# A hybrid attention and convolution layer on one core: V and the third pattern's results in other layouts, and another order at the end of the first attention stretch

## The chip, the cores and the metric

The kernel runs on one core of a Trainium2 chip. The metric is the time of one execution on the device in microseconds (us), lower is better. The core has a matmul engine (TensorE, PE in the profile), a vector engine (VectorE, DVE), a scalar engine (ScalarE, ACT), a general engine (GpSimd, POOL) and a queue that starts transfers (SyncE, SP). ScalarE and GpSimd can start transfers too.

## The reference, cut to what matters

One encoder layer on 2048 positions of width 1024. After a norm, one projection gives queries, keys and values for 8 attention heads of size 64, and two halves for a gated convolution. Each head attends within three patterns (windows of 128 positions at stride 1, 512 at stride 4, 2048 at stride 16), and the three results are weighed by their softmax denominators:

```python
def dilated_sliding_attention(q, k, v):
    outs, lses = [], []
    for window, d in ((128, 1), (512, 4), (2048, 16)):
        half = window // (2 * d)
        o, lse = banded_attention(to_strided(q, d), to_strided(k, d), to_strided(v, d), half)
        outs.append(from_strided(o, d, B)); lses.append(from_strided(lse, d, B))
    w = softmax(stack(lses, axis=0), axis=0)
    return sum(w[..., None] * stack(outs, axis=0), axis=0)

h = x + concat([att, conv]) @ w_out          # att: 8 heads, conv: 31 taps, norm, silu
h = h + cross_attention(rmsnorm(h), rmsnorm(mem))
h = h + square(relu(rmsnorm(h) @ w_up)) @ w_down
out = rmsnorm(h)
```

## The kernel before

Float32 products are formed from high and low parts, three matmuls for each (`mm3`, lines 198 to 200). The work goes by groups of 512 positions (p = 0 to 3), except the projection, which is made for all groups first.

**Scratch in DRAM.** Values of all heads are stored by position (`vtok`, one row of 8 x 130 float16 for each position, with 256 rows of zeros ahead and behind that `edges`, line 711, writes from a tile of 16 partitions; that tile has the tag `raw`, as the weights' tiles have). The results of the second pattern (stride 4) and of the third (stride 16) are stored in `oscr[pair][0]` and `oscr[pair][1]`, a row of two heads by 66 numbers for each position: 64 sums, the denominator and the minimum.

**Attention.** `att_units` (line 948) yields units. A unit writes scores of four blocks of 128 queries and keys into a PSUM bank (kind `S`, L993 and L857), VectorE adds the mask and takes minima (L773), ScalarE takes exponentials (L774), TensorE turns them (L780), ScalarE and VectorE copy the high and low parts (ph L783, pl L784), and TensorE multiplies with V (L788 to L790). `att` (line 1048) runs the three stages of successive units beside one another. The third pattern spans all positions, so it is computed for all groups during group 0's attention (`att_far`, line 837), the *far stretch*; its order for each pair of heads is: head a third pattern, second, first; head b the same. For groups 1 to 3 a pair has first and second pattern only.

V tiles are single: v1 (first pattern, five transfers), v2 (second, eight transfers of 128 pieces), v3 (third, one transfer of 2048 pieces); in the far stretch all three are asked for at a pair's end.

`combine` (line 884) weighs the three results of a pair. It loads the two stored ones (`ld`, lines 889 to 891), waits some steps, and takes the common minimum on VectorE (csm, L904 and L905), exponentials on ScalarE, and the products and sums on GpSimd (L906 to L932). For the last pair of group 0 VectorE does them (`W = DVE if end else POOL`), and its result stays in SBUF as an input of the output projection; the others go through DRAM. `catT` (L940) turns the result. The call `after(st, "dve")` pins the first instruction behind the VectorE instruction written before it.

**The order.** Engines take their instructions in order. The kernel's order is made by generators: `weave(main, (side, rate))` runs `rate` steps of a side for each step of the main one; `pinned` keeps a generator's instructions behind the last one of an engine. A planner then places the instructions on the engines by estimated times. In the far stretch the gate projections of groups 2 and 3 (`rest`) run beside attention, 0.75 step for each attention step. Then group 0's `post` begins: `resid_linear` (line 1182) multiplies the eight chunks of w_out; chunks 0 to 2 run together over inputs 4 to 7 (convolution), 0 and 1, then 2 and 3 (attention pairs), so that the last pair's result is needed last. Their first six steps run beside the last attention units:

```python
    for p in range(NG):
        main = post(p)
        if p == 0:
            weave(islice(pinned(main, "pe"), 6), (first, 2.4))
            drain(first)
        sides = [(att(p + 1), 0.95), (conv(cv, p + 1), 0.6)] if p + 1 < NG else []
        weave(main, *sides)
```

Of the kernel before, what the change touches and what calls it, by code (L numbers as in the profile page):

```python
# [10 lines left out]
F32 = mybir.dt.float32  # L11
# [36 lines left out]
def hybrid_layer(ctx, tc, A, out):  # L48
# [61 lines left out]
    vtok = dr.tile([256 + S + 256, VR], F16, name="vtok")  # L110
# [3 lines left out]
    oscr = [[dr.tile([S, 2 * ROW], F32, name=f"oscr{p}_{q}") for q in (1, 2)] for p in range(4)]  # L114
# [430 lines left out]
    def lin_v(g, ns):  # L545
# [18 lines left out]
        for t in range(4 * ns[0], 4 * ns[-1] + 4):  # L564
# [10 lines left out]
            s2 = st.rearrange("p h e -> p (h e)")  # L575
            gs = slice(g * 4 * VW, (g + 1) * 4 * VW)
            dma(vtok[256 + P * t:256 + P * (t + 1), gs], s2)
# [133 lines left out]
    def edges():  # L711
        zrow = wp.tile([16, 1, VR], F16, tag="raw", name="zrow", bufs=2)
        DVE.memset(zrow, 0.0)
        zb = zrow.to_broadcast([16, 16, VR])
# [122 lines left out]
    def att_far(p2_, h, k, vt, q):  # L837
# [5 lines left out]
        def unit(rq, qh, ql):  # L843
# [39 lines left out]

    def combine(p, pr, o0):

        if p:
            yield
        ld = aq.tile([P, 2, 4, 2, ROW], F32, tag="ld", name=f"ld{p}{pr}")
        for i in range(2):
            dma(ld[:, i].rearrange("p j h e -> p j (h e)"),  # L890
                oscr[pr][i][512 * p:512 * (p + 1)].rearrange("(j p) e -> p j e", p=P))
        yield
        yield
        if p == 0:
            for _ in range(2 if pr < 3 else 1):
                yield
# [3 lines left out]
        end = p == 0 and pr == H // 2 - 1  # L900
# [6 lines left out]
        for i in range(2):  # L907
            W.tensor_tensor(e3[:, 1 + i], mm_, ld[:, i, :, :, HD + 1], op=ALU.subtract)
# [6 lines left out]
        for i in range(2):  # L915
            W.tensor_tensor(d3[:, 1 + i], e3[:, 1 + i], ld[:, i, :, :, HD], op=ALU.mult)
# [8 lines left out]
        for i in range(3):  # L925
            W.tensor_tensor(e3[:, i], e3[:, i], d2, op=ALU.mult)
        at = aq.tile([P, 4, 2, HD], F32, tag="cat", name=f"cat{p}{pr}")
        for i in range(3):
            src = ld[:, i - 1, :, :, 0:HD] if i else o0[:, :, :, 0:HD]
            W.tensor_tensor(src if i else at, src, e3[:, i].unsqueeze(3).to_broadcast([P, 4, 2, HD]), op=ALU.mult)  # L930
            if i:
                W.tensor_tensor(at, at, src, op=ALU.add)  # L932
# [15 lines left out]
    def att_units(p, far, then):  # L948
# [8 lines left out]
        def load_v(pr, pats):  # L957
            es = slice(pr * 2 * VW, (pr + 1) * 2 * VW)
            if 2 in pats and far:
                vt[2] = far.tile([P, 16, 2 * VW], F16, tag="v3", name=f"v3_{pr}")  # L960
                dma(vt[2], vtok[256:256 + S, es].rearrange("(i r) e -> i r e", r=16))
            if 0 in pats:
                vt[0] = aq.tile([P, 5, 2 * VW], F16, tag="v1", name=f"v1_{p}{pr}")
                for c in range(5):
                    t0 = 256 + 512 * p + P * c - 64
                    dma(vt[0][:, c], vtok[t0:t0 + P, es].rearrange("(i r) e -> r i e", r=16))
            if 1 in pats:
                vt[1] = aq.tile([P, 4, 2, 2 * VW], F16, tag="v2", name=f"v2_{p}{pr}")
                for c in range(2):
                    src = vtok[512 * (p + c):512 * (p + c) + 512, es].rearrange("(i a b) e -> b a i e", a=4, b=4)  # L970
                    for b in range(4):
                        dma(vt[1][:, b, c], src[b])

        def unit(pr, hh, pat, g, k, q_, opt, o0):
# [28 lines left out]
            for z in range(2):  # L1003
                blk = 2 * g + z
                for c in range(2):
                    vv = vt[1][:, blk, c] if pat else vt[0][:, blk + c]
# [7 lines left out]
            if g and hh and pat:  # L1014
                dma(oscr[pr][0][512 * p:512 * (p + 1)].rearrange("(p b) e -> p b e", b=4),
                    os_.rearrange("p b h e -> p b (h e)"), POOL if far else nc.scalar)
# [11 lines left out]
        for pr in range(H // 2):  # L1028
            K = [load_keys(2 * pr + hh, p, hh) for hh in range(2)] if far else None
            o0 = aq.tile([P, 4, 2, ROW], F32, tag="o0", name=f"o0_{p}{pr}", bufs=2)  # L1030
            for hh in range(2):
                h = 2 * pr + hh
                if far:
# [3 lines left out]
                    yield from att_far(far, h, k, vt, q3)  # L1037
# [144 lines left out]
    def resid_linear(load, rhs, korder, resid, hs, ssum, key, y, name, steps=False):  # L1182


        for ms in ((0, 1, 2), (3,), (4,), (5,), (6,), (7,)):
            wt = [load(m) for m in ms]
            pts = {}
            for ks in (korder[0:4], korder[4:6], korder[6:8]) if len(ms) > 1 else (korder,):
                for m, (wh, wl) in zip(ms, wt):
                    if m not in pts:  # L1190
                        pts[m] = ps("mm", f"{name}{m}")
# [13 lines left out]
    def post(p):  # L1205
# [9 lines left out]
        def from_x(m):  # L1215
# [8 lines left out]
                                p == 0)  # L1224
# [211 lines left out]
```

## Time and profile before

| | |
|---|---|
| time, median of 3 runs | 2902.63 us (2901.68 to 2903.17) |
| the profiled execution | 2896.44 us; span 2894.6 us, mean granted clock 0.992 |
| TensorE, VectorE, ScalarE, GpSimd busy | 98%, 64%, 40%, 16% of the span |
| transfers | 433.73 MB, mean 150 GB/s |

The profiled execution has its own time beside the runs; the span is from the first instruction to the last. A group line reads: source line, engine, operation, out<-in by the program's names, shapes, count, then busy time and mean, then the engine's idle time before those instructions and who ended it. TensorE's idle time before an instruction stands in brackets in the timeline. The order of phases is: preparation and projections up to 540 us, the far stretch to about 770 us, and then `post` of group 0 with the attention and convolution of group 1 beside, and so on.

### The profile page before, as it was taken

What the parts mean: (1) busy time and instruction counts of PE and PEld (TensorE: products, weight loads), DVE (VectorE), ACT (ScalarE), POOL (GpSimd) and SP (SyncE); (2) the same over time, 40 slices, a digit from 0 to 9 for tenths busy, and PEclk for the clock granted to TensorE, in tenths of its full rate; (3) what the DMA queues carried; (4) which work ended last, traced back from release to release, by engine and by line L of the source; (5) the groups of instructions that cost most, each with busy time, mean ns of one, the idle gap of its engine ahead of it and who ended that gap; (6) DMA issues with size and microseconds to landing.
All of it is one profiled execution on the core that took longest, in us unless ns stands there. A gap on an engine that the chain in (4) does not pass through costs nothing.

```text
span 2894.6 us, 41429 instructions
## 1 busy us (share of the span) xinstructions
PE 2826.2 (98%) x15628; PEld 2377.7 (82%) x15628; DVE 1860.5 (64%) x3311; ACT 1167.0 (40%) x1988; POOL 472.7 (16%) x522
## 2 busy tenths in 40 slices
PE   8989999989899999999999999999999999999999
PEld 7878899878788888888888888888888888888888
DVE  5636536455689876566887756689877555544445
ACT  5623211466444343434543344445333433432233
POOL 1336431133002011200022012002111200000000
PEclk9999999999999999999999999999999999999999
DMA  8979854799834444545444546534543445233332
GB/s 259 295 157 228 200 146 134 178 232 237 219 98 127 142 132 126 170 145 164 124 124 128 146 116 192 175 100 121 143 127 115 139 131 175 90 93 100 97 95 73
DMA packets 606656, 433.73 MB, mean 150 GB/s; under 512 B 174886, under 2 KB 537434, under 8 KB 606457
## 3 DMA queue, kind: packets, MB, share of 16 engines
q1 hardware_dynamic: 566904, 408.81, 49.4%
q10 hardware_dynamic: 37952, 16.88, 2.3%
q0 software_dynamic: 1600, 5.41, 0.7%
q8 instruction: 123, 2.02, 0.3%
q14 instruction: 77, 0.62, 0.1%
HBM read 339.89 MB, written 91.11 MB: 149 GB/s over the span
## 4 chain that ended last, share of the span: by engine, by line
PE 84%; DVE 7%; DMA 4%; issue 2%; ACT 1%; SPq 1%; POOL 0%; POOLq 0%; DVEq 0%; ACTq 0%
PE dn L198 8%; PE dn L199 8%; PE dn L200 8%; PE up L198 8%; PE up L200 7%; PE up L199 7%; PE lin L198 4%; PE lin L200 3%; PE lin L199 3%; PE xs L198 2%; PE xs L200 2%; PE xs L199 2%; PE o L198 2%; PE o L199 2%; PE o L200 2%
## 5 line engine op out<-in xcount | busy, mean ns | idle before, releaser
L199 PE MATMUL dn<-hhl,whi_d 128*128 128x512 f32 (+1 forms) x1056 | 403.0, 384 | 1.4 <-DVE hhl L1310 1.4
L198 PE MATMUL up<-mh,whi_u 128*128 128x512 f32 x1024 | 402.6, 393 | 0.5 <-DVE rl L1307 0.5
L198 PE MATMUL dn<-hhh,whi_d 128*128 128x512 f32 (+1 forms) x1056 | 401.5, 391 | 1.1 <-ACT hhh L1309 1.1
L200 PE MATMUL dn<-hhh,wlo_d 128*128 128x512 f32 (+1 forms) x1056 | 402.1, 384 | 0.0
L199 PE MATMUL up<-ml,whi_u 128*128 128x512 f32 x1024 | 399.7, 390 | 1.6 <-DVE ml L1200 1.6
L200 PE MATMUL up<-mh,wlo_u 128*128 128x512 f32 x1024 | 399.8, 391 | 0.0
L215 DVE SCALAR_TENSOR_TENSOR cacc<-cu,cw,cacc 128x512 f32<-128x512 f32 x480 | 387.9, 808 | 5.5
L189 ACT CAST whi_d<-raw_d 128x1024 fp32r<-128x1024 f32 x128 | 134.6, 1052 | 424.8 <-PE up L199 380.0
L1325 DVE TENSOR_TENSOR h<-h,dn 128x512 f32<-128x512 f32 (+1 forms) x264 | 172.1, 666 | 161.8 <-PE dn L200 160.5
L189 ACT CAST whi_u<-raw_u 128x1024 fp32r<-128x1024 f32 x128 | 134.4, 1050 | 327.7 <-PE dn L199 299.6
L1307 DVE SCALAR_TENSOR_TENSOR rl<-up,ssumx 128x512 f32<-128x512 f32 x128 | 87.9, 690 | 260.6 <-PE up L200 256.4
L198 PEld LDWEIGHTS dn<-hhh,whi_d 128*128 128x128 f32 x1056 | 197.8, 188 | 40.7 <-DVE h L1325 3.5
L200 PEld LDWEIGHTS dn<-hhh,wlo_d 128*128 128x128 f32 x1056 | 198.4, 188 | 39.4
L199 PEld LDWEIGHTS dn<-hhl,whi_d 128*128 128x128 f32 x1056 | 198.8, 188 | 37.6 <-DVE hhl L1310 2.3
L199 PEld LDWEIGHTS up<-ml,whi_u 128*128 128x128 f32 x1024 | 192.5, 188 | 40.8 <-DVE ml L1200 3.0
L200 PEld LDWEIGHTS up<-mh,wlo_u 128*128 128x128 f32 x1024 | 192.3, 188 | 40.1
L198 PEld LDWEIGHTS up<-mh,whi_u 128*128 128x128 f32 x1024 | 192.4, 188 | 38.6 <-DVE rl L1307 0.9
L774 ACT ACTIVATE sm<-sm,o 128x256 f32<-128x256 f32 (+1 forms) x384 | 160.1, 465 | 121.8 <-DVE o L773 121.5
L190 DVE TENSOR_TENSOR wlo_u<-raw_u,whi_u 128x1024 fp32r<-128x1024 f32 x128 | 161.6, 1262 | 26.7 <-ACT whi_u L189 26.5
L190 DVE TENSOR_TENSOR wlo_d<-raw_d,whi_d 128x1024 fp32r<-128x1024 f32 x128 | 161.2, 1260 | 23.5 <-ACT whi_d L189 23.4
L773 DVE CUSTOM_DVE_ANT_0 sm<-s,mask 128x256 f32<-128x256 f32 (+1 forms) x384 | 128.3, 374 | 61.2 <-PE s L993 33.8
L176 POOL TENSOR_TENSOR nr<-st_v,mhalf 128x4 f32<-128x4 f32 (+1 forms) x13 | 13.4, 1031 | 845.7 <-DVE st_v L172 845.7
(402 smaller groups left out, 6341.1 us busy)
## 6 DMA issues: line engine op xcount, KB each, us to landing
raw_u<-in_w_up_dram SPq DMA_DIRECT2D x128, 512.0 KB
raw_d<-in_w_down_dram SPq DMA_DIRECT2D x128, 512.0 KB
raw_o<-in_w_out_dram SPq DMA_DIRECT2D x32, 512.0 KB
raw_a<-ascr SPq DMA_DIRECT2D x32, 512.0 KB
raw_b<-bscr SPq DMA_DIRECT2D x32, 512.0 KB
v<-vtok SPq DMA_DIRECT2D x208, 65.0 KB
k<-kscr SPq DMA_DIRECT2D x24, 512.0 KB
k<-kscr SPq DMA_DIRECT2D x8, 1152.0 KB
```

Source lines behind the costliest of these rows:

```text
L176: POOL.tensor_tensor(dst, v, mhalf.to_broadcast([P, v.shape[1]]), op=ALU.pow)
L189: ACT.copy(hi, raw)
L190: (lo_eng or DVE).tensor_tensor(lo, raw, f(hi), op=ALU.subtract)
L198: PE.matmul(o, lh, rh, start=first, stop=False)
L199: PE.matmul(o, lh, rl, start=False, stop=False)
L200: last["pe"] = PE.matmul(o, ll, rh, start=False, stop=end)
L215: DVE.scalar_tensor_tensor(acc, u[:, t:t + 512], cw[:, c, t:t + 1], acc, op0=ALU.mult, op1=ALU.add)
L773: last["dve"] = DVE.tensor_tensor_reduce(dst, so, mask[:, 256 * m:256 * m + nk], 1.0, 3e38, ALU.add, ALU.min, mn)
L774: last["act"] = ACT.activation(dst, dst, AF.Exp, bias=mn, scale=-1.0)
L1307: last["dve"] = DVE.scalar_tensor_tensor(r, pt, 0.0, rsb, op0=ALU.max, op1=ALU.mult)
L1325: last["dve"] = DVE.tensor_tensor(hs[m][:, sl], hs[m][:, sl], pt, op=ALU.add)
```

## The change

Cut to its core (left out: the same renaming of indices elsewhere, and the argument `done` at its call).

```diff
-    vtok = dr.tile([256 + S + 256, VR], F16, name="vtok")
+    vtok = dr.tile([H // 2, 256 + S + 256, 2 * VW], F16, name="vtok")
-    oscr = [[dr.tile([S, 2 * ROW], F32, name=f"oscr{p}_{q}") for q in (1, 2)] for p in range(4)]
+    oscr = [dr.tile([S, 2 * ROW], F32, name=f"oscr{p}_1") for p in range(4)]
+    ofar = [dr.tile([2, S, ROW], F32, name=f"oscr{p}_2") for p in range(4)]
...
-            dma(vtok[256 + P * t:256 + P * (t + 1), gs], s2)
+            dma(vtok[2 * g:2 * g + 2, 256 + P * t:256 + P * (t + 1)].rearrange("r t e -> t r e"),
+                st.rearrange("p (r h) e -> p r (h e)", r=2))
...
-        zrow = wp.tile([16, 1, VR], F16, tag="raw", name="zrow", bufs=2)
+        zrow = wp.tile([64, 1, VR], F16, tag="raw", name="zrow", bufs=2)
...
-            dma(vtok[t0:t0 + 256].rearrange("(q x) e -> q x e", q=16), zb)
+            dma(vtok[:, t0:t0 + 256].rearrange("r (q x) e -> q r (x e)", q=64), zb)
...
             if rq % 2:
-                dma(oscr[pr][1].rearrange("(p r) (h e) -> p r h e", r=16, h=2)[:, 4 * rq - 4:4 * rq + 4, hh], o2,
-                    POOL)
+                dma(ofar[pr][hh].rearrange("(p r) e -> p r e", r=16)[:, 4 * rq - 4:4 * rq + 4], o2, POOL)
+            if rq == 3:
+                done()
...
+    def load_sum(p, pr):
+        ld = aq.tile([P, 2, 4, 2, ROW], F32, tag="ld", name=f"ld{p}{pr}")
+        ts = slice(512 * p, 512 * (p + 1))
+        dma(ld[:, 0].rearrange("p j h e -> p j (h e)"), oscr[pr][ts].rearrange("(j p) e -> p j e", p=P))
+        for hh in range(2):
+            dma(ld[:, 1, :, hh], ofar[pr][hh, ts].rearrange("(j p) e -> p j e", p=P))
+        return ld
...
-        if p == 0:
-            for _ in range(2 if pr < 3 else 1):
+        end = p == 0 and pr == H // 2 - 1
+        if end:
+            ld = lds[p, pr]
+        else:
+            if p:
+                yield
+            ld = load_sum(p, pr)
+            for _ in range(2 if p else 6):
                 yield
...
-        for i in range(2):
-            W.tensor_tensor(e3[:, 1 + i], mm_, ld[:, i, :, :, HD + 1], op=ALU.subtract)
+        W.tensor_tensor(e3[:, 1:3], mm_.unsqueeze(1).to_broadcast([P, 2, 4, 2]), ld[:, :, :, :, HD + 1],
+                        op=ALU.subtract)
...
-            W.tensor_tensor(src if i else at, src, e3[:, i].unsqueeze(3).to_broadcast([P, 4, 2, HD]), op=ALU.mult)
+        for i, x in ((2, parts[1]), (0, o0[:, :, :, 0:HD]), (1, parts[0])):
+            (POOL if i == 2 else W).tensor_tensor(x if i else at, x, ..., op=ALU.mult)
...
+            q = POOL if p == 1 and pr == 0 else None        # the queue of v1's and v2's loads below
...
             if 1 in pats:
-                vt[1] = aq.tile([P, 4, 2, 2 * VW], F16, tag="v2", name=f"v2_{p}{pr}")
+                vt[1] = aq.tile([P, 2, 4, 2 * VW], F16, tag="v2", name=f"v2_{p}{pr}")
                 for c in range(2):
-                    src = vtok[512 * (p + c):512 * (p + c) + 512, es].rearrange("(i a b) e -> b a i e", a=4, b=4)
-                    for b in range(4):
-                        dma(vt[1][:, b, c], src[b])
+                    dma(vt[1][:, c].rearrange("p b e -> p (b e)"),
+                        vtok[pr][512 * (p + c):512 * (p + c) + 512].rearrange("(i a b) e -> a i (b e)", a=4, b=4), q)
...
-                    os_.rearrange("p b h e -> p b (h e)"), POOL if far else nc.scalar)
+                    os_.rearrange("p b h e -> p b (h e)"),
+                    nc.scalar if not far else (nc.sync if pr == H // 2 - 1 else POOL))
+            if g and hh and pat and far and pr == H // 2 - 1:
+                lds[p, pr] = load_sum(p, pr)
...
                 if pr < H // 2 - 1:
-                    if not far:
-                        load_v(pr + 1, (pat,))
-                    elif not pat:
-                        load_v(pr + 1, (2, 1, 0))
+                    load_v(pr + 1, (pat,))
...
                 for pat in order:
+                    if far and pr == H // 2 - 1 and pat == order[1]:
+                        tail.append((hh, k, qs))
+                        continue
...
+            for hh, k, qs in tail:
+                opt = []
+                yield from [unit(pr, hh, order[1], g, k, qs[order[1]], opt, o0) for g in range(2)]
...
-        for ms in ((0, 1, 2), (3,), (4,), (5,), (6,), (7,)):
+        for ms in ((0, 1, 2, 3) if wide else (0, 1, 2), () if wide else (3,), (4,), (5,), (6,), (7,)):
...
-            for ks in (korder[0:4], korder[4:6], korder[6:8]) if len(ms) > 1 else (korder,):
+            cuts = (0, 4, 6, 7, 8) if wide else (0, 4, 6, 8)
+            for ks in [korder[a:b] for a, b in zip(cuts, cuts[1:])] if len(ms) > 1 else (korder,):
...
         if p == 0:
-            weave(islice(pinned(main, "pe"), 6), (first, 2.4))
+            banks.update(S=(3,), m3=(4,))
+            main_ = pinned(main, "pe")
+            weave(islice(main_, 4), (first, 2))
+            weave(islice(main_, 8), (first, 0.5))
             drain(first)
-        sides = [(att(p + 1), 0.95), (conv(cv, p + 1), 0.6)] if p + 1 < NG else []
+        sides = []
+        if p + 1 < NG:
+            cg = conv(cv, p + 1)
+            if p == 0:
+                cg = chain(pinned(islice(cg, 8), "pe"), cg)
+            sides = [(att(p + 1), 0.95), (cg, 0.6)]
```

`wide` is set for group 0 alone. In words: values are kept by pairs of heads, so that a piece of v2 has 2080 bytes and one of v3 8320, and the transfers of v2 are two for eight; the third pattern's results are kept by heads, stored in pieces of 2112 bytes and loaded in pieces of 264, one load for each head. In the far stretch each V tile is asked for when its own pattern is done. For the last pair the first pattern of both heads comes after both heads' second pattern, and its stored results are loaded at that point. Four chunks of the output projection, not three, run together beside the end, with the score bank of one in the place of two; the fourth takes the freed bank. The zero tile lies on 64 partitions. Group 1's first v1 and v2 come by GpSimd's queue.

More of the change, by code (lines that the diff above doesn't have):

```diff
@@ L835, in far_q, with att_far @@
         return t, ql
-    def att_far(p2_, h, k, vt, q):
+    def att_far(p2_, h, k, vt, q, done):
         pr, hh = divmod(h, 2)
@@ L899, in combine @@
         mm_ = sm_[:, 0].rearrange("p (j h) -> p j h", h=2)
-        end = p == 0 and pr == H // 2 - 1
         W = DVE if end else POOL
@@ L914, in combine @@
         W.tensor_tensor(d3[:, 0], e3[:, 0], o0[:, :, :, HD], op=ALU.mult)
-        for i in range(2):
-            W.tensor_tensor(d3[:, 1 + i], e3[:, 1 + i], ld[:, i, :, :, HD], op=ALU.mult)
+        W.tensor_tensor(d3[:, 1:3], e3[:, 1:3], ld[:, :, :, :, HD], op=ALU.mult)
         dn = sm_[:, 4]
@@ L1036, in att_units @@
                         keys = far_keys(far, h + 1)
-                    yield from att_far(far, h, k, vt, q3)
+                    yield from att_far(far, h, k, vt, q3, lambda: load_v(pr + 1, (2,)) if hh and pr < H // 2 - 1 else None)
                     qs = (q_, q_)
```

41 lines of the change are left out of this document (16 added, 25 removed).

## The prediction

> **What bounds the kernel now.** I read the profile's page first, for the share of each engine; then TensorE's idle time before single instructions, to find where it stands; then the windows of those stretches, the chain that ended last, and the DMA queue's own instructions. The page:
>
> ```profile
> span 2894.6 us, 41429 instructions
> ...
> PE 2826.2 (98%) x15628; PEld 2377.7 (82%) x15628; DVE 1860.5 (64%) x3311; ACT 1167.0 (40%) x1988; POOL 472.7 (16%) x522
> ```
>
> TensorE works in 98% of the span. The change takes no matmul away, so it can win only the 68.4 us in which TensorE is idle, and what TensorE loses by running slowly after a stop. The windows (columns: window, length, busy time of TensorE and of its weight loads, VectorE, ScalarE, GpSimd, then granted clock, DMA share, GB/s) tell where that is:
>
> ```profile
> 180.00:200.00 20.00, 20.00 (x99) 16.66 (x99) 10.05 (x15) 6.39 (x9) 7.63 (x6) 1.00 0.79 129
> 220.00:240.00 20.00, 20.00 (x90) 16.54 (x89) 7.39 (x8) 10.87 (x20) 14.94 (x11) 1.00 1.07 251
> 580.00:780.00 200.00, 172.82 (x1495) 149.74 (x1493) 116.34 (x443) 115.90 (x269) 52.62 (x76) 0.96 0.91 231
> 600.00:620.00 20.00, 16.15 (x127) 14.18 (x126) 8.20 (x34) 8.36 (x22) 7.39 (x18) 0.83 0.87 236
> 620.00:660.00 40.00, 37.64 (x358) 33.88 (x357) 23.14 (x104) 25.09 (x64) 8.77 (x8) 1.00 0.93 228
> 760.00:780.00 20.00, 12.05 (x55) 9.15 (x54) 14.89 (x38) 7.84 (x14) 2.22 (x2) 0.74 0.75 183
> 780.00:860.00 80.00, 80.00 (x427) 66.38 (x426) 63.42 (x118) 37.64 (x72) 3.72 (x3) 1.00 0.37 121
> ```
>
> The far stretch, 580 to 780, holds 27.2 us of idle TensorE; after 780 there is nothing to win, so every edit that acts only there is hidden behind a full TensorE. The longest pieces of the chain that ended last name three places:
>
> ```profile
> 182.88 12.24 DMA vtok<-zrow
> ...
> 752.55 5.03 DMA oscr<-o
> 757.60 3.57 DMA ld<-oscr
> ```
>
> These are the zero rows written around V, and at the far stretch's end the store and then the load of the last pair's results. The change touches both, and a third place in the middle of the far stretch (Part 2).
>
> **Part 1, the zero rows.** The queue and TensorE around them:
>
> ```profile
> 183.56 4.17 SPq L57 DMA_DIRECT2D uscr<-u  x1
> 195.18 0.39 SPq L57 DMA_DIRECT2D raw_k<-in_w_in_dram  x1
> ```
>
> ```profile
> 208.10 1.08 PE L332 MATMUL xt<-ident,xn 128*128 128x128 f32 x4 [7.45 <-DVE xv L337]
> 208.84 0.77 PE L198 MATMUL lin<-xh,whi_kr 128*128 128x512 f32 x1
> 209.41 0.63 PE L199 MATMUL lin<-xl,whi_kr 128*128 128x512 f32 x1
> ```
>
> The tile of zeros lies in a `raw` buffer that the weights raw_k need next, so the SP queue stands from 187.73 (183.56 + 4.17) to 195.18, until both transfers have landed. Behind it wait the stores of x, their buffers, VectorE's copies and at last TensorE's transposes, 7.45 us idle. The change reads the same zeros from 64 partitions, not 16. It can save from 0 (as slow as before) to 7.45 us. Between them: 129 GB/s at a DMA share of 0.79 is 163 GB/s for a full share, and the window 220:240 has 251 / 1.07 = 235; at that rate 12.24 us become 8.5, 3.7 us less. I take 4.5. After the stop TensorE steps 0.57 us from one matmul to the next (208.84 to 209.41), where 0.23 us is usual (759.32 to 759.55 below). With the stop under 3 us I expect that slow stretch gone too (the wait of 2.32 us below has none behind it: its matmuls take 0.20 us, those behind the wait of 3.85 us 0.24); some six slow matmuls at 0.34 us too much make 2 us. **Part 1: 6.5 us.**
>
> The Trainium skill, "SBUF — State Buffer", section "Door 1: The DMA port swizzle", measures 104 GB/s for a transfer on partitions 0 to 15 and 196 on 0 to 63, since a partition's number sets its port. The trace agrees with the first: twice 256 rows of 2,080 bytes in 12.24 us are 87 GB/s. By that page the rows would need half the time, Part 1 would be some 8 us, and the total 1.5 us more.
>
> **Part 2, the combinations of pairs 0 to 2.** VectorE takes the first instruction of a combination, csm, in its order, and stands there until the load has landed. From the answer on the tile csm, what its engine sat idle for (us, times), then TensorE's rows at the same places, then the queue ahead of the first load:
>
> ```profile
>   DMA ld<-oscr: 6.8, 3
>   DMA v<-vtok: 5.4, 1
> ```
>
> ```profile
> 611.77 0.24 PE L790 MATMUL opt<-v,pl 128*128 128x65 f16 x1 [3.85 <-DVE pl L784]
> ...
> 663.57 0.20 PE L790 MATMUL opt<-v,pl 128*128 128x65 f16 x1 [2.32 <-DVE pl L784]
> ...
> 712.21 0.20 PE L790 MATMUL opt<-v,pl 128*128 128x65 f16 x1 [0.74 <-DVE pl L784]
> ```
>
> ```profile
> 593.81 8.08 SPq L57 DMA_DIRECT2D v<-vtok  x8
> ...
> 604.08 0.56 SPq L57 DMA_DIRECT2D ld<-oscr  x1
> ```
>
> TensorE's waits on pl, behind csm in VectorE's queue, make 3.85 + 2.32 + 0.74 = 6.9 us. The load is late because eight V loads stand before it and take 8.08 us of the queue. With V by pairs they are two, and in the new order of SP they stand ahead of the first load, with nothing but qh, ql and a store between. The load should be issued some 6 us earlier, and the combination begins two attention units later (six steps, not four). Added are one load per pair (0.56 us of queue) and 264-byte pieces in it. So all three waits go. The first one's slow stretch goes with it: 600:620 has 127 matmuls in 16.15 us, at the rate of 620:660 (358 in 37.64) they take 13.35, 2.8 us less. **Part 2: 9.7 us**; at worst nothing.
>
> **Part 3, the far stretch's end.**
>
> ```profile
> 759.32 0.39 PE L199 MATMUL o<-catl,whi_o 128*128 128x512 f32 x1
> 759.55 0.39 PE L200 MATMUL o<-cath,wlo_o 128*128 128x512 f32 x1
> ...
> 766.99 0.21 PE L788 MATMUL opt<-v,ph 128*128 128x65 f16 x1 [6.61 <-DMA v<-vtok]
> ...
> 770.03 1.11 PE L940 MATMUL catT<-ident,cat 128*128 128x128 f32 x4 [0.19 <-DVE cat L932]
> 771.93 0.80 PE L198 MATMUL o<-cath,whi_o 128*128 128x512 f32 x1 [0.78 <-ACT cath L942]
> ```
>
> ```profile
> 763.63 0.17 DVE L914 TENSOR_TENSOR csm<-ce,o 128x8 f32<-128x8 f32 x1
> ...
> 768.98 1.00 DVE L932 TENSOR_TENSOR cat<-cat,ld 128x512 f32<-128x512 f32 x1
> ```
>
> ```profile
> oscr<-o POOLq DMA_DIRECT2D x20, 264.0 KB, 6.8
> ```
>
> Here TensorE waits 6.61 us for the next group's first V, then for the combination and its transposes. In the new order the loads of the last pair's results are issued after pattern 1, with the pattern-0 units of both heads and four projection chunks of 12 matmuls still to come; behind the last attention matmul TensorE has 36 more projection matmuls (24 and 12, since the fourth chunk and the finer cut were added) and four transposes before the transposes of cat. That is 36 x 0.23 + 0.6 = 8.9 us. What must be done in it: the combination from csm<-ce,o on, 763.63 to 769.98, 6.4 us, and 0.4 for the copy ahead of it; the minima and the exponentials need no result of these matmuls and come earlier. Margin 2.1 us. The V loads on GpSimd's queue: the third of them is issued some 2 us after the last read, and lands a median 6.8 us later (nearest row, stores of that queue): 8.8 us, where TensorE arrives at 8.9 + 1.1. Margin 1.2 us. So the 6.61 us and the 0.19 go, 6.8 us, and with them the slow stretch: at the rate of 780:860 (427 in 80) the 55 matmuls of 760:780 would take 10.3 us, 1.75 less, and its clock of 0.74 bounds the loss at 5.2; I take 3, as many of the 55 are short. The 0.78 for the copy stays.
>
> What comes new: the third and fourth chunk's weights, and later the fifth's, are cast while the cover that the old third chunk gave (24 matmuls, 5.5 us) is spent; one bank instead of two holds scores; no projection stands between the first units after the last gate matmul. I charge 0.8 us. **Part 3: 9.0 us.**
>
> The Trainium skill, "SBUF — State Buffer", section "Who interferes with whom", speaks against the product that moves to GpSimd: VectorE's instructions with two inputs in SBUF exclude a GpSimd instruction that reads SBUF. No row of this trace shows it by itself. By it the combination ends later by as much as that product lasts, which eats into the margin of 2.1 us and leaves the sum alone; the chance of the first rival below is higher for it.
>
> **Costs nothing.** V's stores in 520-byte pieces, merged GpSimd instructions, the loads of groups 1 to 3, and the convolution tied to TensorE for eight steps: all stand beside a TensorE without a gap (780:860 is full).
>
> **Sum.** 6.5 + 9.7 + 9.0 = 25.2 us. The profiled execution took 2896.4 us (span and 1.8 us around it), so 2871.2; the median of the runs is 6.2 us higher, 2902.6, so 2877.4.
>
> **The rivals.**
> - The end's wait is only exchanged: V on GpSimd's queue or the combination arrives later than the margins of 1.2 and 2.1 us allow, and Part 3 brings nothing. For it: narrow margins. Against: four chunks are more cover than three. 2886.4.
> - VectorE still stands at csm, because the load now waits for the store of pattern 1 at the queue's head: Part 2 is lost. For it: a store lands only after 6.8 us. Against: two units more. 2887.1.
> - Slower: the single score bank. A unit's scores can't be written until VectorE has read the last ones, and nine units run before the second bank is given back. Should each stop TensorE as long as the longest wait of Part 2, 3.85 us, that is 34.7 us: 2912.1. It decides from 25.2 / 9 = 2.8 us a unit. Against: the new order puts a chunk of 12 matmuls (2.8 us) between most units.
> - The change does nothing that can be measured, as other transfers end at the same times: the DMA share of 0.91 in 580:780 speaks for it. 2902.6.
>
> **How the numbers follow.** Forecast 0.63, rivals 0.15, 0.10, 0.06, 0.06. A measurement can tell 0.2%, 5.8 us, from no change. The forecast and the first two rivals are faster; I give 0.03 of them to "same", as two could come together: faster 0.85. Same 0.08, slower 0.07. If everything idle in the three places went (27.2 + 7.45 us and 8 us of slow stretches), it would be 2860; the range begins at 2863 and ends at 2894, above both partial rivals, and leaves out the last two and a little below.
>
> **What would show it.** Right: raw_k on SP near 190, the xt transposes waiting under 3 us; no wait at csm over 1 us; clock 1.00 in every window from 600 on; catT without a stop before it. Wrong: a wait for v of group 1 or cat at the end, scores waiting on VectorE's reads, or new idle time after 780.

## The result and the profile after

The change makes the kernel faster, by a good third of what was forecast: 2893.7 us median of eight runs against 2902.8 for the kernel before, ratio 0.9969 with a 95% interval of 0.9959 to 0.9980. Forecast were 2877.4, with a range from 2863 to 2894; the median lies 0.3 us inside its upper end. The profiled execution took 2888.3 us (before: 2896.4). The page of after:

```profile
span 2886.5 us, 41313 instructions
...
PE 2826.6 (98%) x15628; PEld 2376.2 (82%) x15628; DVE 1857.6 (64%) x3306; ACT 1166.3 (40%) x1988; POOL 458.0 (16%) x469
```

TensorE's work is the same, 2826 us. So the 8 us are idle time, as the prediction said they must be, and the question is which stops went and which came. The windows of after, with the columns of before:

```profile
200.00:220.00 20.00, 16.36 (x65) 13.26 (x66) 9.97 (x13) 9.94 (x14) 13.42 (x13) 0.83 0.77 198
580.00:780.00 200.00, 183.83 (x1534) 159.24 (x1531) 123.55 (x445) 119.39 (x273) 51.20 (x70) 0.97 0.90 241
600.00:620.00 20.00, 20.00 (x195) 18.14 (x194) 13.67 (x58) 12.22 (x32) 7.96 (x14) 1.00 1.03 274
660.00:680.00 20.00, 20.00 (x179) 17.73 (x179) 12.42 (x55) 12.15 (x31) 6.81 (x8) 0.93 1.07 262
760.00:780.00 20.00, 19.28 (x101) 15.73 (x100) 16.93 (x26) 14.09 (x21) 2.16 (x2) 1.00 0.70 199
```

The far stretch has 16.2 us of idle TensorE left of 27.2. Its two worst windows of before, 600 to 620 and 760 to 780, are full, with a clock of 1.00. But 200 to 220 still has a clock of only 0.83 (0.74 in before), and there are new dips, to 0.93 in 660 to 680 and to 0.91 in 700 to 740. TensorE's instructions with a stop of over 1 us before them, beyond the start (in brackets the idle time, and what ended it):

```profile
201.93 0.45 PE L333 MATMUL xt<-ident,xn 128*128 128x128 f32 x1 [2.50 <-DVE xv L338]
205.58 0.45 PE L333 MATMUL xt<-ident,xn 128*128 128x128 f32 x1 [1.71 <-DVE xv L338]
510.45 0.50 PE L199 MATMUL lin<-xh,whi_g 128*128 128x512 f32 x1 [3.12 <-DVE vst L575]
659.20 0.56 PE L857 MATMUL s<-k,ql 128*128 128x256 f32 x1 [2.23 <-DMA ql<-qfar]
705.99 0.39 PE L857 MATMUL s<-k,ql 128*128 128x256 f32 x1 [3.83 <-DMA ql<-qfar]
1082.46 0.77 PE L199 MATMUL dn<-hhh,whi_d 128*128 128x512 f32 x1 [2.42 <-DVE h L1339]
1630.77 0.50 PE L199 MATMUL dn<-hhh,whi_d 128*128 128x512 f32 x1 [1.30 <-DVE h L1339]
2178.84 0.50 PE L199 MATMUL dn<-hhh,whi_d 128*128 128x512 f32 x1 [2.41 <-DVE h L1339]
```

Left out are two stops of 1.18 and 1.39 us, at 588.62 and 730.49, that before has in like size, a new one of 1.18 us at 743.24 for the cast weights wlo_o, and the last two of the kernel. Six of these eight are new: 3.12, 2.23, 3.83 and the three before dn. All the predicted ones are smaller or gone: 7.45 us became 2.50; the waits for pl behind csm, the 6.61 at the end and the 0.19 before catT do not appear.

How much each place brought is read by taking the same TensorE instruction in both traces and subtracting its start in after from its start in before. Between stops this lead is constant to some hundredths of a us wherever TensorE's order is the same in both, so most steps in it have one place:

| stretch of before, us | lead of after at its end, us | change in it | predicted |
|---|---|---|---|
| 0 to 200 (not touched by the change) | 1.2 | +1.2 | 0 |
| 200 to 240, zero rows | 6.35 | +5.1 | 6.5 |
| at 513, V copies | 2.97 | -3.4 | 0 |
| 520 to 960, far stretch and its end | 15.15 | +12.2 | 18.7 |
| 960 to the end, groups 0 to 2 | 7.9 | -7.3 | 0 |

The first row is chance: in the traces of the experiments below the lead over before at 190 us, before any edit shows, lies between -1.2 and 2.8.

Within the far stretch the lead can be read at places where TensorE's order is the same in both traces:

| place in before, us | lead, us | what lies between |
|---|---|---|
| 600 | 2.96 | |
| 668 | 12.80 | the first two combinations, +9.8 |
| 675 | 9.59 | the wait for ql at 659 in after, -3.2 |
| 712 | 11.40 | the third combination, +1.8 |
| 742 | 5.61 | the wait for ql at 706 in after, -5.8 |
| 818 | 15.69 | the end, +10.1 |

So the combinations bring 11.7 us (forecast 9.7) and the end 10.1 (9.0), and two new waits for queries, with the slow clock behind them, take 9.0 of it back.

In the last row of the first table the three stops before dn take 4.3, 1.6 and 2.6 us; other small steps bring 1.2.

### The profile page after: what moved, and what is told of

Read it like the earlier page. It is cut to its first block, busy times and chain, and to the rows that moved or that the text cites. A ratio compares the mean times of both kernels' runs of the same rounds, so it can differ in the third digit from the quotient of the medians.

```text
span 2886.5 us, 41313 instructions
## 1 busy us (share of the span) xinstructions
PE 2826.6 (98%) x15628; PEld 2376.2 (82%) x15628; DVE 1857.6 (64%) x3306; ACT 1166.3 (40%) x1988; POOL 458.0 (16%) x469
## 4 chain that ended last, share of the span: by engine, by line
PE 82%; DVE 9%; DMA 5%; issue 2%; ACT 2%; POOL 1%; SPq 1%; POOLq 0%; DVEq 0%; ACTq 0%
PE dn L199 8%; PE dn L200 8%; PE dn L201 8%; PE up L199 7%; PE up L200 7%; PE up L201 7%; PE lin L199 4%; PE lin L201 4%; PE lin L200 4%; DVE cacc L216 3%; PE o L199 2%; PE o L200 2%; PE o L201 2%; PE xs L199 2%; PE xs L201 2%; PE xs L200 2%
## 5 line engine op out<-in xcount | busy, mean ns | idle before, releaser
L1339 DVE TENSOR_TENSOR h<-h,dn 128x512 f32<-128x512 f32 (+1 forms) x264 | 172.3, 667 | 162.9 <-PE dn L201 161.7
```

Of the source, the lines that this page charges most:

```text
L1339: last["dve"] = DVE.tensor_tensor(hs[m][:, sl], hs[m][:, sl], pt, op=ALU.add)
```

## The experiments

Times are medians; ratios are to the kernel before, run beside it on the same chip, with their 95% interval.

**The zero rows alone.** `edges` of before with the tile on 64 partitions:

```diff
-        zrow = wp.tile([16, 1, VR], F16, tag="raw", name="zrow", bufs=2)
+        zrow = wp.tile([64, 1, VR], F16, tag="raw", name="zrow", bufs=2)
...
```

> The kernel before with one part of the change alone: the tile of zeros on 64 partitions. By the trace of after, in which the two transfers of zeros took 7.06 us instead of 12.24: TensorE's wait of 7.45 us before the transposes becomes 2.5, the second one of 1.8 stays, and the time falls by 5 us (ratio 0.9983). By the prediction's term of 6.5 us, with the slow stretch behind the wait gone: 0.9978, and a clock of 1.00 in 200 to 220 us. Rival: the saving in after came from other parts (SP's queue ahead of it), and alone it gives nothing: 1.000.

Measured: 2896.7 us, ratio 0.9988 (0.9979 to 0.9997). TensorE's stop is 2.22 us, as in after, and the lead behind it grows by 4.5. So the saving is this edit's own, and not the queue's. The expected second stop stays too, at 2.27. In this trace the lead is lost again later: where before had a stop of 2.32 us in the far stretch, this run has 5.33, and 7.05 for 6.61 at the end.

```profile
200.82 0.30 PE L332 MATMUL xt<-ident,xn 128*128 128x128 f32 x1 [2.22 <-DVE xv L337]
...
659.14 0.24 PE L790 MATMUL opt<-v,pl 128*128 128x65 f16 x1 [5.33 <-DVE pl L784]
...
765.48 0.21 PE L788 MATMUL opt<-v,ph 128*128 128x65 f16 x1 [7.05 <-DMA v<-vtok]
```

**The stops before dn.** `h` (L1339) is late there because VectorE stood still before it. In order of time, in after, the V loads of SP, the store on ScalarE's queue, and VectorE's next mask instruction; then the same three in before:

```profile
1070.02 1.14 SPq L57 DMA_DIRECT2D v<-vtok  x2
1070.83 0.33 ACTq L57 DMA_DIRECT2D oscr<-o  x1
1077.92 0.42 DVE L773 CUSTOM_DVE_ANT_0 sm<-s,mask 128x256 f32<-128x256 f32 x1 [5.21 <-PE dn L201]
```

```profile
1085.20 5.76 SPq L57 DMA_DIRECT2D v<-vtok  x8
1086.01 0.33 ACTq L57 DMA_DIRECT2D oscr<-o  x1
1090.28 0.42 DVE L773 CUSTOM_DVE_ANT_0 sm<-s,mask 128x256 f32<-128x256 f32 x1 [2.39 <-DMA oscr<-o]
```

The mask instruction also writes minima into the tile that the store reads, of which there is one, so it waits for the store to land: 4.3 us after its issue in before, 7.1 in after. (The view names the dn matmul there, which ended at about the same time; in four of the six such waits of after it names the store.) In before the store is issued behind two of eight V transfers, and the others are issued while it runs; in after it is issued behind both transfers of 260 KB. Two experiments part this from other causes: one gives the store's tile a second buffer, the other splits the V transfers again.

```diff
-                o1[0] = (far if far and pr % 2 == 0 else aq).tile([P, 4, 2, ROW], F32, tag="o1", name=f"o1_{p}{pr}")
+                o1[0] = (far if far and pr % 2 == 0 else zp if p and pr % 2 else aq).tile(...)
...
-    top.tile([P, 296], F32, name="tpad")
+    top.tile([P, 184], F32, name="tpad")
```

> After, with a second buffer for the second pattern's results in groups 1 to 3 (and 448 bytes of padding less for it), so that the next pair need not wait for the store of the last. Theory A (the store lands 2.7 us later than before because it stands behind the two large V transfers, VectorE waits for it, and TensorE for VectorE): the waits of 2.42, 1.30 and 2.41 us before the matmuls of dn at 1082, 1631 and 2179 us go, and 6 to 8.5 us with them (ratio to before 0.994, where after has 0.997). Theory B (VectorE is late there because of the pinned convolution or the loads in 264-byte pieces): the waits stay within 1 us of what they were, 0.997.

```diff
...
+                    if p:
+                        for b in range(4):
+                            dma(vt[1][:, c, b], src.rearrange("(i a b) e -> b a i e", a=4, b=4)[b], q)
...
```

> After, with the second pattern's V of groups 1 to 3 loaded in eight transfers of 520-byte pieces, as before, from the new layout. Theory A (the burst of two transfers of 260 KB delays the store issued behind it): the store lands 4.1 to 4.4 us after its issue as before, not 6.8 to 8.1, the three waits before dn go, 6 to 8.5 us less than after (0.994 to before). Theory B (the pinned convolution or the 264-byte loads): the store may land sooner, the waits stay, 0.997. Theory C (the store is slow because of other large transfers, the MLP's weights): neither changes.

Measured with the split: 2881.6 us, ratio 0.9934 (0.9920 to 0.9947), 12 us below after's median (10 by the ratios); in the traces the lead over after grows by 9.0 us behind 960. At the three places the store, issued at 1070.80 in the first, now lands after 4.1 to 4.4 us:

```profile
1075.24 0.42 DVE L773 CUSTOM_DVE_ANT_0 sm<-s,mask 128x256 f32<-128x256 f32 x1 [2.57 <-DMA oscr<-o]
```

Of TensorE's waits between 900 and 2450 us, in after (first) and in this kernel, the row of h goes:

```profile
PE dn L199 <- DVE h L1339: 6.1, 3, 2.4
PE dn L200 <- DVE hhl L1324: 1.1, 2, 0.6
PE dn L199 <- ACT hhh L1323: 1.1, 2, 0.5
PE up L200 <- DVE ml L1214: 0.9, 1, 0.9
```

```profile
PE up L200 <- DVE ml L1218: 1.7, 3, 0.7
PE dn L200 <- DVE hhl L1328: 1.1, 2, 0.6
PE dn L199 <- ACT hhh L1327: 1.1, 2, 0.5
```

The pinned convolution and the loads in 264-byte pieces are unchanged there, so they are not the cause. With the second buffer the store still lands some 7 us after its issue, the three stops go as well, but the time is 2900.0 us, ratio 0.9994 (0.9985 to 1.0003): the lead shrinks steadily, with no stop over 1.3 us, from 10.6 us at 818 to -7.5 at the end. The next experiment shows where a part of that comes from.

**Padding alone.** After, with only the second hunk of the edit above, 448 bytes less of padding:

> After with nothing changed but the padding tile that stands first among the buffers on the right side, 184 numbers long instead of 296, so that all buffers there lie 448 bytes elsewhere; the order of every engine is the same. In the run with the second buffer, which had this too and 2112 bytes more in another pool, the matmuls of lin, xs and up stepped 236, 237 and 233 ns instead of 232, 233 and 229, and the time drifted up by 15 us after 900 us. Theory A (the buffers' addresses do it, and this shift is the cause): the same steps, and 10 to 25 us more than after (ratio to before 1.000 to 1.005). Theory B (the other pool's 2112 bytes, or something else there): steps and time of after, 0.997.

Measured: 2902.9 us, ratio 1.000 (0.999 to 1.001), 9 us above after (5.9 in the traces), with every engine's order as in after and with its stops, but for the one of 2.23 us for ql at 659. A late window of after (first) and of this kernel tells why:

```profile
2600.00:2800.00 200.00, 200.00 (x882) 164.72 (x881) 93.70 (x110) 59.32 (x73) 0.00 (x0) 1.00 0.33 98
```

```profile
2600.00:2800.00 200.00, 200.00 (x876) 163.77 (x875) 94.39 (x111) 58.54 (x71) 0.00 (x0) 1.00 0.32 95
```

TensorE is busy throughout, at full clock, and does 876 matmuls where it did 882; from 240 to 380 us, full in both too, 615 where it did 624. In these windows the buffers' addresses alone make it 0.7 to 1.5% slower. It is not the chip either: in the traces of the twelve kernels here with 296 numbers of padding, from both chips that the experiments ran on, the two windows hold 624 to 627 and 880 to 882. Theory A holds, a little under its price. In the run with the second buffer, which takes 2112 bytes more in another pool as well, it was 870 in the window shown; that the rest of its loss comes from addresses too is likely, and not shown.

**The stop at 510.** VectorE in after, and in before:

```profile
502.97 0.69 DVE L239 TENSOR_TENSOR lsum<-lc 128x512 f32<-128x512 f32 x1 [8.46 <-DMA lc<-cscr]
```

```profile
507.30 0.69 DVE L238 TENSOR_TENSOR lsum<-lc 128x512 f32<-128x512 f32 x1 [1.99 <-DMA lc<-cscr]
```

In VectorE's order of after, the first sum over lc stands ahead of the copies of V's tiles 11 and 12; in before it stands behind the 11th. With two issues instead of eight the planner expects the loads of lc earlier and moves their users up; against TensorE's work they land no earlier, and the copies, whose banks TensorE needs, stand behind.

> After, with the second pattern's V of the first pair of group 0 alone loaded in eight transfers of 520-byte pieces. By the order of VectorE's instructions the first sum over lc then stands two V copies later, as before. Theory A (with two issues instead of eight the planner places the loads of lc, and with them that sum, ahead of V copies that TensorE's banks need, while the loads land no sooner): VectorE's wait for lc falls from 8.5 to about 2 us, TensorE's wait of 3.12 us before the gate matmul at 510 us goes, and the time by 3.4 us (ratio to before 0.9957). Theory B (the copies are late because the V stores in 520-byte pieces hold their tiles): the wait of 3 us stays.

The edit is the one of the split, with `if not p and not pr`. Measured: 2883.0 us, ratio 0.9939 (0.9919 to 0.9958). VectorE's wait for lc is 3.94 us, TensorE's stop before the gate matmul is gone, and the lead runs through this place unchanged (4.88). The store of V in 520-byte pieces is as in after, so theory B falls. So the cause is shown; the price is not measured well. The median lies 10.7 us under after's, but three of the five runs are at 2881 to 2883 us and two at 2890 to 2892, and the one that was traced, 2890.3, is not under after's 2888.3: it loses 3 us against it near 1630, where its stop before dn is 2.79 us. The 3.4 us are read from the step in the lead alone.

**The waits for ql.** SP's queue in after, ahead of the wait at 705.99:

```profile
693.65 7.42 SPq L57 DMA_DIRECT2D v<-vtok  x4
701.12 0.60 SPq L57 DMA_DIRECT2D ql<-qfar  x1
```

Four small V loads hold the queue for 7.4 us, since each issue waits for the transfer eight issues earlier, among them the large ones: the second is issued at 696.53, when the V transfer issued at 684.18 has landed (696.51). Two experiments moved the loads to GpSimd's queue: first the queries', then the V loads'; a third gave the end its old order.

```diff
+            dma(f(d), f(qfar[...].rearrange("d r i -> d (r i)")), POOL if h > 3 and not e else None)
```

> After, with the first half of the queries for the third pattern of heads 4 to 7 loaded by GpSimd's queue, not SP's. Theory A (SP's queue: these loads are issued behind V loads that each wait until the transfer eight issues earlier has landed): TensorE's waits of 2.23 and 3.83 us for ql at 659 and 706 us go, and 6 to 8 us with the slow matmuls behind them (0.9945 to before). Theory B (the DMA engines themselves are full, share 0.83 to 1.07 there): the loads land as late as before, the waits stay above 1.5 and 3 us. Possible cost: GpSimd's products of the combination stand behind a load that waits for TensorE, and the first pair's catT is later.

Measured: 2897.8 us, ratio 0.9989 (0.9980 to 0.9998), slower than after. The waits for ql went, and one of 4.04 us for qh (before the scores at 718.95) and one of 1.19 behind the first combination came.

```diff
-                    dma(vt[0][:, c], vtok[pr][t0:t0 + P].rearrange("(i r) e -> r i e", r=16), q)
+                    dma(vt[0][:, c], vtok[pr][t0:t0 + P].rearrange("(i r) e -> r i e", r=16), POOL if far and pr > 1 else q)
```

> After, with the first pattern's V of pairs 2 and 3 of group 0 loaded by GpSimd's queue behind the store there; TensorE's order is the same to the last instruction, and on SP's queue the load of ql follows its qh at once. Theory A (SP's queue: ql stands behind five V loads, each of which waits for an older large transfer to land): the waits of 2.23 and 3.83 us for ql go below 0.5, and with the slow matmuls behind them the time falls by 6 to 8 us (ratio to before 0.9945). Theory B (the DMA engines are full there): ql is issued earlier and lands no earlier, the waits stay above 1.5 us. Theory C: the waits go and are given back at the far stretch's end or before, since V comes later.

Measured: 2891.3 us, ratio 0.9967 (0.9954 to 0.9980), the same as after. The wait of 2.23 us for ql became one of 1.50 for pl. The wait of 3.83 is now for the next load in the queue:

```profile
694.42 3.77 SPq L57 DMA_DIRECT2D raw_o<-in_w_out_dram  x1
698.28 6.20 SPq L57 DMA_DIRECT2D qh<-qfar  x2
...
705.90 0.35 PE L856 MATMUL s<-k,qh 128*128 128x256 f32 x1 [2.85 <-DMA qh<-qfar]
```

Neither theory A nor B is quite right: ql came in time, and the place went to a weight load, behind which the next query waited. It is theory C, the wait is handed on. What the Trainium skill says agrees ("DMA: Bandwidth & Descriptors", section "Issuing engines are not separate DMA queues": another issuing engine saves only the time of issuing).

```diff
-                    if far and pr == H // 2 - 1 and pat == order[1]:
+                    if False:
...
-                                p == 0, p == 0)
+                                p == 0)
...
-            banks.update(S=(3,), m3=(4,))
-            main_ = pinned(main, "pe")
-            weave(islice(main_, 4), (first, 2))
-            weave(islice(main_, 8), (first, 0.5))
+            weave(islice(pinned(main, "pe"), 6), (first, 2.4))
```

> After, with the old order at the far stretch's end: first patterns after each head's second, three projection chunks, two score banks, the old weave. The new layouts, the early load of the last results and group 1's V on GpSimd's queue stay. Theory A (the end's order is worth 9 us, as forecast, but it also takes the scores of head 7 ahead of the load of ql, 3.83 us): a stop of 5 to 7 us comes back at the end with slow matmuls behind it, the wait for ql at 706 us goes, and the sum is 4 to 6 us more than after (ratio to before 0.999). Theory B (the wait for ql is a matter of the queue alone): the wait stays, and the sum is 8 to 10 us more than after (1.000).

Measured: 2903.8 us, ratio 1.0004 (0.9995 to 1.0013), 10.1 us above after. No wait for ql is left in the far stretch: with the first patterns of head 6 back in their place, the scores of head 7 come later, and the load is in time. (The wait at 659 lies ahead of the edited places; it is missing in the run with the padding alone too, so it comes and goes.) At the end there are two stops again:

```profile
754.21 0.21 PE L788 MATMUL opt<-v,ph 128*128 128x65 f16 x1 [5.57 <-DMA v<-vtok]
...
761.78 0.47 PE L947 MATMUL catT<-ident,cat 128*128 128x128 f32 x1 [4.97 <-DVE cat L939]
```

Theory A was right on both stops. Its price of 4 to 6 us fits what the trace shows by 960 us, 7.6 lost against after, of which 2.4 go to a granted clock of 0.50 from 588 to 595, ahead of the edited places; the rest of the 10 lies behind, where the stops before dn are longer in this run (2.76, 3.31 and 2.62 us).

**Was it the queue or the two steps?** Against TensorE's work the last load of each combination is issued only 1.4, 0.1 and 3.3 us earlier in after (599.66, 646.97 and 692.17 us, where before has 604.08, 656.90 and 706.01, less the lead of about 3, 9.8 and 10.5). So the two added steps were tried alone, on before, and taken out, of after:

```diff
-            for _ in range(2 if pr < 3 else 1):
+            for _ in range(4 if pr < 3 else 1):
```

> The kernel before with one number changed: the combinations of pairs 0 to 2 in the far stretch wait six steps after their loads, not four; V stays by position and in eight transfers. In after the loads are issued only 1.4, 0.1 and 3.3 us earlier against TensorE's work than before, not the 6 that the prediction took. Theory A (the two steps took the waits at csm away, not the queue): VectorE's waits at csm of 5.44, 3.19 and 2.19 us fall under 1, TensorE's stops of 3.85, 2.32 and 0.74 go, and the far stretch gains 7 to 10 us (ratio 0.997). Theory B (the eight V transfers ahead of the load): the waits stay above 2 us, ratio 0.999 or more.

```diff
-            for _ in range(2 if p else 6):
+            for _ in range(2 if p else 4):
```

> After with the combinations four steps after their loads, as before; all else as in after. Theory A (the two steps): VectorE waits at csm again, 2 to 5 us at two or three of the places, TensorE stops behind it, and the time is 4 to 8 us above after's (ratio to before 0.999). Theory B (V by pairs took the queue's time away): the waits stay under 1 us and the time is after's, 0.997.

The steps on before: 2905.9 us, ratio 1.0011 (1.0002 to 1.0020). The waits at csm are under 0.9 us, just as theory A has it, and the time is 3.5 us longer. TensorE's waits from 580 to 780 us, the largest in before, in after and in this kernel in turn, show the exchange (us in total, times, longest):

```profile
PE opt L790 <- DVE pl L784: 13.9, 14, 3.9
PE opt L788 <- DMA v<-vtok: 6.6, 1, 6.6
```

```profile
PE opt L790 <- DVE pl L784: 6.1, 8, 1.4
PE s L857 <- DMA ql<-qfar: 6.1, 2, 3.8
```

```profile
PE opt L788 <- DMA v<-vtok: 12.1, 4, 7.8
PE opt L790 <- DVE pl L784: 6.8, 9, 1.2
PE s L856 <- DMA qh<-qfar: 2.1, 1, 2.1
...
PE s L857 <- DMA ql<-qfar: 1.6, 3, 0.7
```

In place of the waits at csm, the steps alone leave TensorE waiting elsewhere: it arrives at the next V and queries before they have landed. The window 580 to 740 of before, after and this kernel:

```profile
580.00:740.00 160.00, 141.51 (x1302) 124.47 (x1300) 91.49 (x378) 99.88 (x238) 47.52 (x71) 0.98 0.94 240
```

```profile
580.00:740.00 160.00, 145.73 (x1314) 127.94 (x1311) 90.99 (x379) 99.93 (x240) 42.51 (x61) 0.97 0.96 256
```

```profile
580.00:740.00 160.00, 142.82 (x1264) 124.70 (x1262) 89.87 (x374) 96.41 (x232) 46.19 (x70) 0.94 0.98 232
```

The DMA engines are busy at 0.94 to 0.98 in all three. After moves 256 GB/s at that, the two kernels with the old layouts 232 to 240. The larger pieces of v2 are not needed for it: the last kernel below, with v2 in 520-byte pieces again, moves 256 GB/s there as well, at 0.96.

After with four steps: 2900.6 us, ratio 0.9991 (0.9982 to 1.0000), 6.9 above after. VectorE waits at csm again, 2.98 us at 607.64 and 4.23 at 655.77, and TensorE stops for 3.36 at 657.84. So the two steps take the waits away. On before they cost 3.5 us, in after they bring 6.9: something else in the change turns them into time. Whether that is the other layouts or the new order in which V is asked for is not shown, as no run has either alone.

**The stalls mended.** Second pattern's V in eight transfers, except in pairs 1 to 3 of the far stretch; first pattern's V of pairs 2 and 3 by GpSimd's queue; zeros from 128 partitions:

> After with all three stalls mended: second pattern's V of groups 1 to 3 and of the first pair in eight transfers, first pattern's V of pairs 2 and 3 on GpSimd's queue; and the zeros from 128 partitions, with 1040 bytes in a piece. If the three are independent: 2881.6 (measured with the first alone) less 3.4 and 6 to 8, so 2870 to 2872, ratio to before 0.989 to 0.990. If the zeros are bound by the number of source partitions, their transfers take under 5 us; if by HBM or the pieces, 7 us or more. Rival: the far stretch's waits are exchanged for others, and the time stays near 2880.

Measured: 2873.6 us, ratio 0.9901 (0.9886 to 0.9916). TensorE has no stop before dn, none at 510, 1.49 for pl at 656 instead of 2.23, and 2.41 and 0.78 us at 700 instead of 3.83. VectorE waits at csm once, 2.81 us at 654.51. Raw_k is issued 5.5 us after the first zeros (182.34 to 187.83), where it was 7.9 in after (181.00 to 188.88) and 13.0 in before (182.14 to 195.18). So the zeros did follow the number of partitions, though not under 5 us.

> The mended kernel (2873.6 us, 0.9901) with every load of the second pattern's V in eight transfers, so that of V only the third pattern's keeps its large pieces. Theory A (two transfers for eight bring nothing in the far stretch either): 2871 to 2876, ratio 0.990, waits at csm under 1 us. Theory B (they free SP's queue there): waits at csm and ql of 2 to 5 us come back, 2878 to 2885, ratio 0.992 to 0.994.

With eight transfers in every pair: 2871.1 us, ratio 0.9895 (0.9882 to 0.9909). Theory A: the two transfers for eight bring nothing that can be measured. This is the fastest version, 31 us under before and 22.6 under after. One wait at csm of 2.71 us is in its trace, against that theory's 1, as the kernel before it has one too; TensorE's stop behind it is 1.40, and its longest in the far stretch 3.05, before the scores with qh at 695.83.

## Why the prediction was right and wrong

**What bounds the kernel, and where.** Right. TensorE's work is the same, and the gain is idle time. The three places were the right ones to win at. What failed is that nothing was put down for new stops outside them and between them.

**Part 1, 6.5 us.** The lead grows by 5.1. The transfers' term was 4.5 and measures 4.95 (7.45 to 2.50). The step that failed is the slow stretch: "With the stop under 3 us I expect that slow stretch gone too". The clock is 0.83 in 200 to 220, and just behind the stops of 2.50 and 1.71 us it is 0.50. The rule was taken from two stops of before, 2.32 and 3.85 us, and two are too few. The stretch's size of 2 us was about right: in the fastest version above the clock is 1.00 behind a stop of 2.09 us, and the lead over before grows there by 9.6 us, against 7.4 in the mended one, with 0.53 behind a stop of 2.05. The Trainium skill's rates ("SBUF — State Buffer", section "Door 1: The DMA port swizzle"), by which Part 1 would be some 8 us, have 1.9 times as much from 64 partitions as from 16; in the chain of after the zero rows take 7.06 us, which is 151 GB/s for 87 in before, 1.7 times as much.

**Part 2, 9.7 us.** The waits behind csm went, all three, and their places bring 11.7 us of lead; the first alone 6.8, for 3.85 + 2.8 in the forecast. The reason was wrong in part: "The load should be issued some 6 us earlier" measures 1.4, 0.1 and 3.3; the two steps did it. The term that failed is what comes new, which was put at one more load and its small pieces: it did not ask what is late next. That was queries, 2.23 and 3.83 us with a granted clock of 0.51 and 0.68 in the 3 us behind them, 9.0 us of lead, on DMA engines that were at 0.91 already. That share was read, and used only as the rival that nothing happens.

**Part 3, 9.0 us.** Right in mechanism: no stop for V, cat or catT at the end, 0.72 us for the copy, clock 1.00. The place brings 10.1 us of lead by 818. Undone, it costs 10.1 us by the medians, of which its trace shows some 5 by 960, since the wait for ql goes with it. Both margins held, and the rival with the single score bank fell: from 740 to 860 us TensorE's waits are 1.2 us for wlo_o, 0.7 for cath, and 0.2 for VectorE's reads of scores. What was missed is its other side: moving head 6's first patterns to the end brings head 7's scores forward, past what its queries' load allows, 3.83 us. The prediction counted what comes later by the move, not what comes earlier.

**"Costs nothing".** This is the step that failed at the highest price, 3.4 and 7.3 us: "all stand beside a TensorE without a gap (780:860 is full)". A full TensorE says that nothing is late now, not by how much it may be later. Before had VectorE waiting 2.39 us for the same store at 1090.28, and the addition that TensorE needs 2.9 us behind that; both were in the trace, and were not read. And the two transfers for eight were weighed as a saving of SP's time alone. They are also 520 KB at once ahead of whatever is issued next, and a shorter time in the planner's reckoning, which moved VectorE's instructions.

**Rivals and range.** The first two rivals did not happen: the end has no stop for V or cat, and VectorE does not stand at csm. That the second's size, 9.7 us less, is near what the far stretch fell short by together with the copies at 513 (18.7 to 8.8) is chance. The rival that nothing happens for want of DMA was right for two steps alone, not for the change. Faster, which had 0.85, came out. That the range holds the median, by 0.3 us, is luck: its end was set above the two partial rivals, and not for losses at 510, at ql and behind 960, which are what happened. Of the signs set down, raw_k near 190 (188.88), the short waits of xt, csm and catT came; the clock of 1.00 from 600 on did not, and one sign of being wrong did, new idle time after 780.

## What to carry to other kernels

Where the DMA engines are nearly full, a wait that is taken away comes back as the next transfer's: price it by what lands next. The same two steps cost 3.5 us in one kernel here and brought 6.9 in the other. Fewer and larger transfers are not free where a small one is issued behind them and an engine waits for it; look for stores that free a single buffer. Behind a full bottleneck look up how long the engines that feed it already wait, for that is the slack that an edit "off the path" spends.

## What was not expected of the hardware

Moving buffers by 448 bytes, nothing else, made TensorE 0.7 to 1.5% slower at full clock in the two windows read, and the kernel 9 us slower, as much as the whole change brought; why an address does this, no run here shows. And the granted clock does not follow the length of the stop alone: in after it was 0.51 in the 3 us behind a stop of 2.42 us (1082.46), 0.57 behind one of 1.39 (730.49), 1.00 behind one of 2.41 (2178.84), and 1.00 behind one of 3.12 (510.45). The Trainium skill ("TensorE: Matmul & The Clock Gate", "What's actually happening") has half the clock after an idle window of about 3.4 us; here shorter stops sufficed and a nearly as long one did not.
